# Forming layer 1's third adaLN group on VectorE behind the delta-rule stages instead of in layer 0's second feed-forward product

## The chip, the cores and the metric

The kernel is one program on one core of a Trainium2 chip. The metric is the device time of that core in microseconds, the median of three runs. Engines are called TensorE (PE in the rows, its weight loads PEld), VectorE (DVE), ScalarE (ACT), GpSimd (POOL) and SyncE (SP, which here only issues DMAs).

## The reference

One inference step through two trunk layers, on 128 context tokens and 512 latent tokens of width 1024, all in float32. Cut to what matters here:

```python
mod = (jax.nn.silu(cond) @ p['w_ada'] + p['b_ada'])[:, None, :]
sh1, sc1, gt1, sh2, sc2, gt2 = jnp.split(mod, 6, axis=-1)
h = rmsnorm(x, p['g_pre_mix']) * (1.0 + sc1) + sh1
...  # h @ w_in; gated delta rule, HGRN2 and latent attention side by side -> mix
x = x + gt1 * rmsnorm(mix @ p['w_out'], p['g_post_mix'])
h = rmsnorm(x, p['g_pre_ffn']) * (1.0 + sc2) + sh2
ff_a, ff_b = jnp.split(h @ p['w_ffn_in'], 2, axis=-1)
x = x + gt2 * rmsnorm((jax.nn.silu(ff_a) * ff_b) @ p['w_ffn_out'], p['g_post_ffn'])
```

`cond` is one vector for the latent tokens and one for the context. So `mod` is a product of two rows with a 1024 x 6144 matrix, 24 MB per layer. The kernel cuts it into three groups of 2048 columns: group 0 is sh1 and sc1, group 1 is gt1 and sh2, group 2 is sc2 and gt2.

## The kernel before

The residual stream is kept feature-major (128 partitions x 8 blocks x 640 tokens), and the tokens are worked in two halves of 320. Every large product is made of matmuls of 128 x 128 weights on 320 columns: a weight is split into a high and a low part in a reduced float32 format (ScalarE makes `wh`, VectorE `wl`, lines 632 and 633), and each 128 x 128 block costs three matmuls per half (line 656). Projections drain through two pairs of PSUM banks, tags g0 and g1.

The instructions are not ordered by hand. The code says what depends on what, and its order is a priority; a planner then simulates the engines, starts on each engine the ready instruction of the highest priority, and so fixes each engine's queue and the places of tiles in rings of buffers. `high_priority(offset=...)` lifts weights (WPRI) and some drains ahead of the code's order. On the chip each engine runs its queue strictly in order. A tile of tag "r" is a region of 128 x 2 x 640 float32; there are 12 of them (`BUFS`, line 39), and 8 of tag "h". A new tile waits until one of its tag is released.

A layer (`layer`, line 1371) runs its mixer first. `ORDER` (line 46) is `g0 g1 i0|2*e0 i1+L0|2*m0+e1 P0|f0 a0|m1+f1`: the two delta-rule halves (`gdn`, g0 and g1), the projections of the HGRN2 halves (i0, i1) and of the latent attention (L0), then the rest. In layer 1 the first HGRN half's tokens of half 0 are projected ahead of everything. A delta-rule half (`gdn_raw`, `gdn_main`) takes two region tiles (KQ and VT), forms its projections and convolutions (line 740), sends a triangular matrix through DRAM into another layout and back (lines 848 to 873), and then scans over chunks (lines 946 to 969), each step with small matmuls on TensorE and short operations on VectorE in turn. KQ lives until the scan's end, VT until the half's last step (`gdn_end`). `hgrn_in(1)` takes four region tiles (two for itself, two for the latent attention) if they haven't been taken. Then comes the output projection, the first feed-forward product (a seven-product scheme, line 563) and the second (w_ffo, pieces of both halves for the first four of eight output blocks, then half by half).

The adaLN groups are formed in two ways. `ada` uses TensorE, and `ada_vec` (line 269) uses VectorE: for each of four blocks j of 512 columns it loads eight weight tiles of 128 x 512, two to a DMA of 512 KB (four DMAs per block, line 293), into a ring of VRING = 2 tiles, and multiplies each by a per-partition scalar and adds it to an accumulator, for the two conditions in turn (line 297 the first, line 299 the other seven). Two accumulators of the same size alternate. `total` (line 279) then sums an accumulator over its 128 partitions with eight matmuls of one column, in two bursts; a float32 matmul makes two records. After the fourth block, `ada_end` makes the gains and gates. It is a generator that stops after each block; a block's `total` is written behind the next block's accumulation. Before the change, layer 0 forms its own groups 1 and 2 on TensorE (`GR`), and layer 1's group 0 too (`PE_NEXT`); layer 1's groups 1 and 2 (`VEC_NEXT`) go through `ada_vec` with "h" tiles, two blocks ahead of each of the first four output blocks of layer 0's second feed-forward product (line 1479).

Of the kernel before, what the change touches and what calls it, by code (L numbers as in the profile page):

```python
# [50 lines left out]
SPRI = 5000  # L51
NKEEP = 6
GR = ((1, 2), ())
PE_NEXT, VEC_NEXT = (0,), (1, 2)
VRING = 2
MPRI = 8000
HPRI = 0
# [109 lines left out]
class Builder:  # L167
# [1203 lines left out]
    def layer(self, l, h, pre):  # L1371
# [3 lines left out]
        inp = lambda n, halves=(0, 1): pre.pop(n) if n in pre else self.gemm(I["w_in"][l, n], hv, KD, halves)  # L1375
        filler = self.ada(l, GR[l], "c1", "w1", AD0) if GR[l] else iter(())
        fill = lambda n: [next(filler, None) for _ in range(n)]
        rb = lambda shape: self.blk(shape, tag="r")
        r2 = rb([128, 2, NT])
        self.mkab = r2[:, 1]  # L1380
# [10 lines left out]
        def gdn(pr):  # L1391
            self.use(f"c{pr}", f"w{pr}")
            gd[pr] = (rb([128, 2, NC, 64]), rb([128, 2, NT]))
            self.gdn_raw(l, pr, inp, *gd[pr])
            if pr == 0:
                fill(100)
            terms[pr] = self.gdn_main(l, pr, *gd[pr])

        def gdn_end(pr):
            self.use(f"c{pr}", f"w{pr}")  # L1400
            KQ, VT = gd[pr]
            yield from self.mix_out(VT[:, 0], terms[pr])
            mix[pr] = self.finish_mixer(VT[:, 0], VT[:, 1], self.vec[:, l, V_GNW:V_GNW + 1], f"w{pr}")
# [25 lines left out]
        def hgrn_end(pr):  # L1429
            self.use(f"c{pr}", f"w{pr}")  # L1430
            yield from self.mix_out(hs[pr][0][:, 0], terms[2 + pr])
            mix[2 + pr] = self.finish_mixer(hs[pr][0][:, 0], hs[pr][2], self.vec[:, l, V_HNW:V_HNW + 1], f"w{pr}")

        steps = {"g": gdn, "e": gdn_end, "i": hgrn_in, "m": hgrn, "f": hgrn_end, "L": lambda n: mla_in(), "P": lambda n: mla(),
                 "a": lambda n: self.attention(l, st[1], mix, range(4))}
        for group in ORDER.split():
# [187 lines left out]
```

## Time and profile before

| | |
|---|---|
| Median of 3 runs | 1977.1 us (1975.47 to 1982.02) |
| Profiled execution | 1979.4 us, span 1977.6 us, mean granted TensorE clock 0.99 |
| TensorE matmul, weight load | 97%, 88% of the span |
| VectorE, ScalarE, GpSimd | 69%, 50%, 1% |
| DMA | mean 115 GB/s; 32 loads of 512 KB for `ada_vec` |

Stages of the profiled execution: layer 0's mixer to about 500 us, its output projection and first feed-forward product to about 860, its second product to about 1062; layer 1's mixer to about 1458, its products to the end. Times in the rows are microseconds from the span's start, means of one instruction are nanoseconds. An engine that is busy need not be at its peak: matmuls are pipelined and their ends are modelled, so that a matmul which waits inside the array looks longer. The granted clock is a share of TensorE's full 2.4 GHz.

### The profile page before, as it was taken

What the parts mean: (1) busy time and instruction counts of PE and PEld (TensorE: products, weight loads), DVE (VectorE), ACT (ScalarE), POOL (GpSimd) and SP (SyncE); (2) the same over time, 40 slices, a digit from 0 to 9 for tenths busy, and PEclk for the clock granted to TensorE, in tenths of its full rate; (3) what the DMA queues carried; (4) which work ended last, traced back from release to release, by engine and by line L of the source; (5) the groups of instructions that cost most, each with busy time, mean ns of one, the idle gap of its engine ahead of it and who ended that gap; (6) DMA issues with size and microseconds to landing.
All of it is one profiled execution on the core that took longest, in us unless ns stands there. A gap on an engine that the chain in (4) does not pass through costs nothing. (4 is left out here: it accounts for less than half of the span.)

```text
span 1977.6 us, 40034 instructions
## 1 busy us (share of the span) xinstructions
PE 1910.7 (97%) x15688; PEld 1739.2 (88%) x15688; DVE 1370.9 (69%) x2962; ACT 997.1 (50%) x2086; POOL 16.2 (1%) x64
## 2 busy tenths in 40 slices
PE   6999999999999999999999999999999999999996
PEld 3748888888999979999998987888899999999996
DVE  5537567696677757788887786678756977776245
ACT  4515253754676435551355551648457755555243
POOL 0000000000000000000000000000000000000000
PEclk9999999999999999999999999999999999999998
DMA  9652211210554452256764232112036532223344
GB/s 320 207 183 64 59 42 28 58 37 18 187 176 150 139 166 85 86 167 202 235 192 133 62 100 52 29 42 58 5 100 187 167 117 86 86 86 103 87 139 141
DMA packets 157486, 226.56 MB, mean 115 GB/s; under 512 B 38769, under 2 KB 65521, under 8 KB 157297
## 3 DMA queue, kind: packets, MB, share of 16 engines
q1 hardware_dynamic: 156656, 222.70, 36.8%
q8 instruction: 123, 2.02, 0.4%
q0 software_dynamic: 640, 1.31, 0.3%
q14 instruction: 67, 0.54, 0.1%
HBM read 209.99 MB, written 12.65 MB: 113 GB/s over the span
## 5 line engine op out<-in xcount | busy, mean ns | idle before, releaser
L632 ACT ACTIVATE wh<-raw 128x512 fp32r<-128x512 f32 (+2 forms) x634 | 391.0, 617 | 603.8 <-PE g L656 413.5
L633 DVE TENSOR_TENSOR wl<-raw,wh 128x512 fp32r<-128x512 f32 (+1 forms) x610 | 408.2, 671 | 303.4 <-ACT wh L632 265.9
L656 PE MATMUL g<-h,wh 128*128 128x320 f32 x2448 | 541.4, 319 | 8.6 <-ACT h L481 3.3
L656 PEld LDWEIGHTS g<-h,wh 128*128 128x128 f32 x2448 | 401.3, 189 | 41.0 <-issue 16.2
L656 PE MATMUL g<-h,wl 128*128 128x320 f32 x1224 | 338.3, 316 | 0.5 <-DVE wl L633 0.5
L656 PE MATMUL g<-w,wh 128*128 128x320 f32 x1152 | 246.1, 314 | 5.5 <-ACT r L1448 5.5
L656 PEld LDWEIGHTS g<-h,wl 128*128 128x128 f32 x1224 | 218.4, 189 | 12.0 <-issue 6.4
L656 PEld LDWEIGHTS g<-w,wh 128*128 128x128 f32 x1152 | 191.0, 191 | 6.2 <-ACT r L1448 6.0
L656 PE MATMUL g<-r,wh 128*128 128x320 f32 x768 | 165.5, 313 | 0.0
L656 PE MATMUL g<-w,wl 128*128 128x320 f32 x480 | 132.7, 314 | 0.0
L563 PE MATMUL g<-h,wh 128*128 128x320 f32 x768 | 129.0, 310 | 0.0
L656 PEld LDWEIGHTS g<-r,wh 128*128 128x128 f32 x768 | 127.5, 190 | 0.6
L563 PEld LDWEIGHTS g<-h,wh 128*128 128x128 f32 x768 | 116.3, 188 | 3.6 <-issue 3.4
L557 DVE TENSOR_TENSOR raw<-raw,raw 128x512 f32<-128x512 f32 x128 | 88.0, 687 | 2.2
L656 PEld LDWEIGHTS g<-w,wl 128*128 128x128 f32 x480 | 87.4, 192 | 0.2
L563 PE MATMUL g<-w,wh 128*128 128x320 f32 x512 | 85.9, 310 | 0.0
L563 PE MATMUL g<-r,wh 128*128 128x320 f32 x512 | 85.5, 309 | 0.0
L299 DVE SCALAR_TENSOR_TENSOR h<-h,silu_c,h 128x512 f32<-128x512 f32 x112 | 78.5, 745 | 4.6 <-DMA h<-in_w_ada_dram 4.5
L563 PEld LDWEIGHTS g<-w,wh 128*128 128x128 f32 x512 | 77.6, 188 | 3.4 <-ACT r L575 3.4
L656 PE MATMUL g<-r,wl 128*128 128x320 f32 x288 | 79.3, 312 | 0.0
L563 PEld LDWEIGHTS g<-r,wh 128*128 128x128 f32 x512 | 77.7, 188 | 0.0
L563 PE MATMUL g<-h,wl 128*128 128x320 f32 x384 | 71.9, 309 | 0.0
(378 smaller groups left out, 3094.8 us busy)
## 6 DMA issues: line engine op xcount, KB each, us to landing
raw<-in_w_ffi_dram SPq DMA_DIRECT2D x224, 256.0 KB
raw<-in_w_ffo_dram SPq DMA_DIRECT2D x120, 256.0 KB
raw<-in_w_in_dram SPq DMA_DIRECT2D x106, 256.0 KB
w<-in_w_ada_dram SPq DMA_DIRECT2D x96, 256.0 KB
raw<-in_w_out_dram SPq DMA_DIRECT2D x64, 256.0 KB
h<-in_w_ada_dram SPq DMA_DIRECT2D x32, 512.0 KB
r<-in_w_ada_dram SPq DMA_DIRECT2D x32, 256.0 KB
r<-in_xT_dram SPq DMA_DIRECT2D x6, 640.0 KB
```

What stands on the lines that cost most here:

```text
L299: nc.vector.scalar_tensor_tensor(out=acc[:, s], in0=raw[:, k % 2], scalar=c, in1=acc[:, s], op0=ALU.mult, op1=ALU.add)
L557: nc.vector.tensor_tensor(out=o, in0=a, in1=b, op=ALU.add)
L563: nc.tensor.matmul(ps, lhsT=w[e][:, k], rhs=a[f][:, k], start=first and i == 0, stop=i == 11, skip_group_check=not first)
L632: self.nc.scalar.activation(hi, src, AF.Copy)
L633: self.nc.vector.tensor_tensor(out=lo, in0=src, in1=hi.bitcast(F32), op=ALU.subtract)
L656: self.nc.tensor.matmul(ps[h], lhsT=w[:, k], rhs=rhs(e, kk, h), start=(kk == 0 and i == 0), stop=(kk == nk - 1 and i == 2))
```

## The change

Layer 1's group 2 leaves `VEC_NEXT` and is formed inside layer 1's own mixer, by the same `ada_vec`, with tiles of tag "r" in place of "h" and PSUM of tag c1 in place of c0. The generator is advanced by two blocks behind the first delta-rule half's `gdn_main`, and to its end behind the second's. As the generator makes its tiles at its first step, they come behind the tiles of the first half and before those of the second in the code's order. No arithmetic changes.

```diff
 GR = ((1, 2), ())
-PE_NEXT, VEC_NEXT = (0,), (1, 2)
+GV = ((), (2,))
+PE_NEXT, VEC_NEXT = (0,), (1,)
 VRING = 2
@@
         fill = lambda n: [next(filler, None) for _ in range(n)]
+        slow = self.ada_vec(l, GV[l], "c1", "r") if GV[l] else iter(())
         rb = lambda shape: self.blk(shape, tag="r")
@@
             terms[pr] = self.gdn_main(l, pr, *gd[pr])
+            for _ in range((2, 100)[pr]):
+                next(slow, None)
```

## Rows read from the trace of the kernel before

**Rows 1.** The page: engines' busy us, and the chain that ended last

```profile
PE 1910.7 (97%) x15688; PEld 1739.2 (88%) x15688; DVE 1370.9 (69%) x2962; ACT 997.1 (50%) x2086; POOL 16.2 (1%) x64
...
PE 27%; DVE 2%; ACT 1%; issue 1%; DVEq 0%; ACTq 0%
```

**Rows 2.** PE, PEld, DVE, ACT, POOL busy us (instructions), clock, DMA, GB/s

```profile
870.00:1005.00 135.00, 131.94 (x907) 130.13 (x906) 113.69 (x196) 35.74 (x68) 0.00 (x0) 0.98 0.70 218
1100.00:1300.00 200.00, 194.54 (x2185) 167.71 (x2185) 143.68 (x359) 94.10 (x200) 3.59 (x9) 1.00 0.22 56
1195.00:1237.00 42.00, 42.00 (x426) 32.99 (x428) 26.24 (x99) 6.82 (x14) 0.00 (x0) 1.00 0.20 50
...
1808.50:1943.50 135.00, 134.98 (x919) 134.56 (x918) 53.71 (x91) 46.90 (x88) 0.00 (x0) 1.00 0.43 125
```

**Rows 3.** The same view for the matmuls of line 656 alone

```profile
870.00:1005.00 135.00, 119.74 (x779) 0.98 0.70 218
...
1808.50:1943.50 135.00, 134.58 (x917) 1.00 0.43 125
...
1195.00:1237.00 42.00, 30.63 (x145) 1.00 0.20 50
```

**Rows 4.** Lines that form groups; timeline rows: start, us, operation, count

```profile
L299 DVE SCALAR_TENSOR_TENSOR h<-h,silu_c,h x112: 739/744/754, 871.1 to 1001.3; 128x512 f32<-128x512 f32 x112
...
L282 DVE TENSOR_TENSOR mods<-m,vec x8: 155/157/167, 888.5 to 1004.1; 128x8 f32<-128x8 f32 x8
...
L293 SPq DMA_DIRECT2D h<-in_w_ada_dram x32: 367/368/427, 848.5 to 993.5; - x32
...
891.44 3.39 DVE L299 SCALAR_TENSOR_TENSOR h<-h,silu_c,h 128x512 f32<-128x512 f32 x5
...
935.75 0.88 DVE L297 TENSOR_SCALAR h<-h,silu_c 128x512 f32<-128x512 f32 x2
```

**Rows 5.** TensorE's timeline around one burst, and its waits from 945 to 1010

```profile
983.08 1.02 PE L279 MATMUL m<-onet,h 128*128 128x1 f32 x8 [0.42 <-DVE h L299]
983.96 0.54 PE L656 MATMUL g<-r,wh 128*128 128x320 f32 x2
...
PE m L279 <- DVE h L299: 1.3, 3, 0.7
```

**Rows 6.** TensorE alone behind two bursts: busy us (matmuls), granted clock

```profile
919.00:923.00 4.00, 4.00 (x19) 0.59 0.72 236
...
1003.50:1008.00 4.50, 4.50 (x23) 0.62 0.21 58
```

**Rows 7.** ScalarE's timeline, first drains of the second HGRN half

```profile
1183.05 0.77 ACT L671 ACTIVATE r<-g 128x320 f32<-128x320 f32 x2
...
1198.01 0.77 ACT L671 ACTIVATE r<-g 128x320 f32<-128x320 f32 x2
```

**Rows 8.** Timelines: last statistic, a convolution; line 949 of the first scan

```profile
1062.64 0.81 PE L445 MATMUL m<-w,onesD 128*128 128x320 f32 x2 [0.47 <-DVE w L441]
...
1130.92 0.88 DVE L740 SCALAR_TENSOR_TENSOR w<-w,vec,w 128x642 f32<-128x642 f32 x1
...
L949 DVE SCALAR_TENSOR_TENSOR st_r<-m,eg,r x20: 272/276/284, 1196.0 to 1233.9; 128x64 f32<-128x64 f32 x20
```

**Rows 9.** Stretches as in rows 2; gap: length less DVE

```profile
1065.00:1120.00 55.00, 52.77 (x347) 48.93 (x347) 35.19 (x73) 31.59 (x74) 2.16 (x12) 0.94 0.19 55
1120.00:1190.00 70.00, 67.46 (x541) 61.58 (x541) 58.68 (x122) 38.08 (x88) 1.74 (x3) 1.00 0.33 84
1190.00:1212.00 22.00, 21.21 (x338) 16.68 (x335) 14.09 (x48) 4.70 (x10) 0.00 (x0) 1.00 0.17 49
1212.00:1237.00 25.00, 25.00 (x262) 19.77 (x264) 14.41 (x59) 2.56 (x5) 0.00 (x0) 1.00 0.25 59
```

**Rows 10.** The chain of waits, a run of small matmuls

```profile
1378.21 1.47 PE m L1040 x32
```

**Rows 11.** VectorE's timeline, layer 1, the first use of G2

```profile
1502.45 2.87 DVE L514 SCALAR_TENSOR_TENSOR w<-w,G,w 128x320 f32<-128x320 f32 x6 [1.56 <-ACT w L407]
```

## The prediction

> **What bounds the kernel now.** I read the engine totals first: TensorE is busy for 97% of the span, VectorE for 69%, and the chain of work that ended last is almost all matmul [rows 1]. Whatever moves VectorE work can therefore pay only where TensorE waits for VectorE, and can cost where it makes TensorE wait. Next come the stretches of the table by stage [rows 2]: 870 to 1005 us is the part of layer 0's second feed-forward product beside which groups 1 and 2 of layer 1 are formed; 1808.5 to 1943.5 is the same product in layer 1 with no such work beside it; 1100 to 1300 holds layer 1's two delta-rule stages and 1195 to 1237 the state scan of the first. Matmuls of the product alone in the first two, of equal length, are 779 and 917 [rows 3]. At 135 us / 917 = 0.147 us each, the forming of two groups takes 138 x 0.147 = 20.3 us of TensorE's time. Half of that is what the change touches. The delta-rule stretch has TensorE busy for 194.5 of 200 us, but it is looser than that: the scan's 145 projection matmuls fill 30.6 us [rows 3] where 145 x 0.147 = 21.3 would do. VectorE is busy for 113.7 of 135 us in the first stretch and 143.7 of 200 in the stages that shall take the work [rows 2].
>
> **Part 1, what leaves the feed-forward product.** Group 2 is half of the 112 + 16 VectorE operations [rows 4]. Five of the long ones in a row take 3.39 us, so each follows the last by (3.39 - 0.745)/4 = 0.66 us; two of the short ones take 0.88, 0.44 each. With seven small ones of 0.16 (line 282 four times and three gains and gates) that is 56 x 0.66 + 8 x 0.44 + 1.1 = 41.6 us of VectorE. With it go half of the 32 loads of 512 KB, and the small sums over partitions of line 279. VectorE is not the engine that ends this stretch, so its 41.6 us alone give nothing. What lies on TensorE is this. Each of a group's four blocks has two bursts of eight records; a burst begins at 983.08 and the next matmul at 983.96 [rows 5], 0.88 us. 8 x 0.88 = **7.0 us** go. TensorE waits for VectorE ahead of these bursts, **1.3 us** from 945 us on [rows 5]. And behind the last burst the granted clock is 0.62 from 1003.5 to 1008 (the level of 1.2 GHz for most of it): 23 matmuls where 4.5/0.147 = 30.6 fit, so 7.6 x 0.147 = **1.1 us**; the same followed group 1's third block at 919 [rows 6], and that one stays. Sum: -9.4 us.
>
> **Part 2, what the delta-rule stages get.** The same 7.0 us of bursts arrive there. TensorE's queue is in order and 97% busy, so I take the whole: **+7.0**, with bounds 0 (all of it in the scan's looseness above) and 7.0. The waits ahead of the bursts come along: **+1.3**, bounds 0 and twice that, 2.6, since here the scan's own VectorE operations stand in the queue too. For a half-clock stretch I take 0 (the clock is 1.00 from 1100 to 1300 [rows 2]), at most 1.1.
>
> The loads: 16 issues of 0.37 us on SP's queue [rows 4], among the projection weights and the delta rule's round trip through DRAM (lines 848 to 873). The stretch moves 56 GB/s and 8.4 MB over 200 us add 42, against 218 in the stretch that they leave [rows 2], so the transfers cost nothing. A load that waits for its ring tile holds everything behind it on SP for at most one tile's four operations, 2.7 us; the weights have seven buffers of lead, the round trip has none. I take 0, upper bound 2.7 for each of two round trips that run while the sums are formed.
>
> The VectorE operations between the scan's steps: the planner lets a ready operation start in any gap. An operation of 0.66 us holds a scan step back by 0.33 on average. Ten steps with three hand-overs each are 30 places, so 10 us at most if every place is hit, and nothing as long as TensorE has projection matmuls to run meanwhile. I take **+1**, bounds 0 and 10.
>
> **The region buffers.** The tag "r" has 12 buffers. At the first projection of the second HGRN half (i1) they hold r2, hg, hs0 (2), the delta rule's KQ and VT of both halves (4): 8, and i1 takes the last four. After the change the slow sums hold four from before the second half's KQ and VT are made until they end, so all 12 are taken and i1's first two tiles must wait for a release. It wants them at 1183.1 and at 1198.0 us [rows 7]. When do they come free? Nothing but tiles and loads holds the sums back, so I let them start when the product has given up its tiles, some us behind its last statistic at 1062.6, and fill VectorE's gaps. That the planner fills gaps ahead of program order, the rows show: a convolution of the second half (line 740) runs at 1130.9, and the first half's scan, which the code writes earlier (line 949), from 1196.0 [rows 8]. The gaps are 19.8 us from 1065 to 1120, 11.3 to 1190, 7.9 to 1212, 10.6 to 1237 [rows 9]. Three blocks (31 us) fit by about 1190, when the first accumulator comes free, and all four (41.6) by about 1218. i1's first tile is thus late by 7 us and the second, when a ring tile is done with, by about 15. TensorE feels this only when both pairs of PSUM banks (tags g0, g1) are full: with the first projection drained at about 1190 the third can run, and the fourth waits some us for the second to drain. I take **+2**. Lower bound 0, for a later tile gives nothing back. Upper bound: the scan runs with no projection beside it. Then the 21.3 us of projection wait, the scan shrinks to 42 - 21.3 = 20.7 us, of which its own 426 - 145 = 281 small records [rows 2, 3], at 1.47/32 = 0.046 us each [rows 10], fill 12.9; 7.8 us of TensorE are lost.
>
> The group's results are first used in layer 1 at line 514, at 1502 us [rows 11], 280 us after they would be done: nothing.
>
> **Sum.** -9.4 + 7.0 + 1.3 + 1 + 2 = +1.9 us. The profiled execution took 1979.4 us (span 1977.6), 2.3 above the median of 1977.1; so 1981.3 for a run like it, and 1979.0 as a median.
>
> **Rivals.** A measurement of this kernel can tell about 0.3%, 5.9 us, from no change.
>
> A, slower: the buffers decide. If the third block isn't done by about 1205, no tile comes free, both bank pairs are full from 1197 and TensorE has only the scan. That happens if VectorE's gaps are fewer than I count, as blocks 3 and 4 stand behind the second delta-rule half, beside which VectorE is busy for 58.7 of 70 us from 1120 to 1190 [rows 9]. Price: 7.8 us (above) and up to 8 more, as the scan then has no cover for the operations between its steps (24 of 0.33). -9.4 + 8.3 + 7.8 to 15.8 = +6.7 to +14.7, **about 1988**. For it: 16 tiles want 12 places. Against: the first release suffices, and KQ goes when the scan ends in any case. The Trainium skill's Perfetto Trace Analysis, section Optimization Strategy, says that a gap that keeps returning on the engine that should be saturated can mean that there isn't room for the next tile. No such gap is in the trace before the change; by that rule the change would make one. Chance 0.30.
>
> B, faster: the bursts and their waits fall into the looseness of the scans (30.6 us of matmul time for 21.3 of work). Then -9.4 stays nearly whole, **about 1969**. For it: the weight loads fill 167.7 of 200 us in the delta-rule stretch and 130.1 of 135 in the product [rows 2]. Against: TensorE can't jump over an instruction that waits. The Trainium skill's Perfetto Trace Analysis, section Identifying the Most-Contended Engine, says to judge TensorE's room by the busy share of its weight loads and not by that of its matmuls; by that rule 16% of this stretch would be free and the 8.3 us would vanish. The trace agrees that the matmul share hides some slack, as the counts show, but not that a burst can use it. Chance 0.20.
>
> C, the change doesn't do what it says: the sums wait for nothing but tiles, so the planner draws them ahead of the delta-rule stages, to 1065 to 1120, where VectorE has 19.8 us of gaps beside norm and gates, and the rest is done before i1 asks at 1183. No hold, no scan disturbed: -9.4 + 8.3 = -1.1, **1976**. Against: 41.6 us don't fit into 31.1. Chance 0.10.
>
> **How the numbers follow.** Forecast 0.40, A 0.30, B 0.20, C 0.10. The range of 80% reaches from 1968 (B with a little less than all hidden) to 1990 (A without its last third); it leaves out some 0.08 on either side. Faster by over 0.3% (below 1971.2): most of B and a tail of the forecast, 0.20. Slower (above 1983.0): A and a tail of the forecast from its open bounds, 0.34. Within: 0.46.
>
> **What would show it.** In the product from 945 to 1005: no line 299 or 279, about 69 matmuls in 10 us, no stretch at the lower clock at 1004. Layer 1's first projection about 9 us earlier. Line 299 with "r" tiles in layer 1: if its third block ends by 1205 (on the old clock) the forecast holds, if all end before 1183 it is C; if the third block runs on into the end of the first scan and TensorE's projection matmuls in that scan are far fewer than 145, it is A. If the bursts appear in the scans and the stretch from the first projection to the attention doesn't grow by 7 us, it is B. I am wrong altogether if the planner reorders something else, such as the conversion of weights, by more than these few us.

## The result and the profile after

| | before | after |
|---|---|---|
| time, median (lowest to highest), us | 1979.6 (1975.5 to 1984.3) | 2011.3 (2007.8 to 2011.7) |
| ratio, 95% interval | 1 | 1.0149 (1.0133 to 1.0165) |
| profiled span, us | 1977.6 | 2006.0 |

The change makes the kernel slower by 1.5%. The prediction said 1979.0, with 1990 as its upper end, so both the time and the range were wrong. Differences in us below are (ratio - 1) x 1979, with the interval worked out likewise, so the change is +29.5 (26.3 to 32.7). One profiled execution can stand several us from the next: the last statistic of layer 0's product, up to which e7 and e13 (below) run the same code, ends at 1048.1 us in the one and at 1057.2 in the other.

After the change TensorE has as many matmuls as in [rows 1] and is busy longer, at a smaller share. Line numbers of after are one higher up to line 1378. From the page of the changed kernel:

```profile
PE 1918.9 (96%) x15688; PEld 1749.0 (87%) x15688; DVE 1373.9 (68%) x2962; ACT 999.3 (50%) x2086; POOL 16.3 (1%) x64
```

To see where the time is, cut layer 1's mixer at its events. In the changed kernel these are the switch of ScalarE's table at the end of the gates (1095.6), the first scan (1196.1 to 1228.0), the second scan (1266.1 to 1301.8) and the last projection drained (1391.2). Columns as in [rows 2]:

```profile
1095.60:1196.10 100.50, 86.00 (x777) 78.26 (x777) 85.91 (x163) 44.78 (x94) 3.68 (x12) 0.92 0.44 128
1196.10:1228.00 31.90, 20.83 (x234) 15.34 (x231) 26.60 (x96) 4.12 (x14) 0.00 (x0) 0.55 0.18 47
1228.00:1266.10 38.10, 37.34 (x569) 33.34 (x571) 23.39 (x49) 22.35 (x41) 0.00 (x0) 0.91 0.17 40
1266.10:1301.80 35.70, 35.70 (x532) 29.38 (x528) 27.07 (x91) 10.85 (x24) 0.00 (x0) 1.00 0.08 26
1301.80:1391.20 89.40, 85.13 (x791) 74.99 (x791) 62.10 (x135) 51.27 (x116) 1.47 (x2) 0.94 0.21 61
```

The same five stretches in the kernel that leaves the group out (e5 below), which has the change's gain and none of its work in the mixer:

```profile
1096.00:1180.00 84.00, 80.96 (x770) 72.60 (x768) 64.52 (x134) 47.65 (x106) 3.59 (x9) 1.00 0.31 79
1180.00:1218.20 38.20, 38.20 (x357) 29.88 (x357) 25.49 (x97) 6.40 (x13) 0.00 (x0) 1.00 0.18 52
1218.20:1241.10 22.90, 22.65 (x481) 20.22 (x480) 12.58 (x24) 14.76 (x28) 0.00 (x0) 1.00 0.13 27
1241.10:1284.90 43.80, 42.52 (x518) 35.24 (x519) 33.00 (x99) 20.48 (x43) 0.00 (x0) 1.00 0.11 31
1284.90:1346.80 61.90, 59.68 (x708) 50.61 (x707) 47.93 (x108) 43.36 (x96) 1.47 (x2) 1.00 0.18 53
```

Both start within half a microsecond of each other. From there the changed kernel needs 295.6 us, the other 250.8. Of the 44.8 us between them, TensorE's idle time (length less PE busy) is 30.6 - 6.8 = 23.8, and 21.0 is TensorE being busy longer. The totals' own time is 7.0 of that; for the rest there is the granted clock. A mean between 0.5 and 1 mixes the two levels, so a stretch of length T at mean c spends 2(1 - c)T at 1.2 GHz: 16.1 + 28.7 + 6.9 + 0 + 10.7 = 62 us in the changed kernel, none in the other.

Three things are seen in the trace of after. **The first scan has no projections beside it**: line 657's matmuls, 145 in [rows 3], are none from 1190 to 1220, and i1's drains, at 1183 and 1198 in [rows 7], begin at 1227.57, as that scan ends and its KQ comes free.

```profile
1190.00:1220.00 30.00, 0.00 (x0) 0.00 (x0) 0.62 0.18 44
1220.00:1240.00 20.00, 3.34 (x11) 2.04 (x11) 0.64 0.14 38
```
```profile
1227.57 0.77 ACT L672 ACTIVATE r<-g 128x320 f32<-128x320 f32 x2 [16.07 <-PE m L947]
```

**The totals run behind the second scan.** From TensorE's timeline: the second and third follow the second scan's last product (line 955), though the third block's sums end at 1220. The accumulators are held until these totals have run, and the fourth block's sums come only behind them (to 1325).

```profile
1302.02 0.45 PE L955 MATMUL m<-st_r,w 64*64 64x64 f32 x8
1302.39 1.95 PE L280 MATMUL m<-onet,r 128*128 128x1 f32 x16
...
1305.01 2.29 PE L280 MATMUL m<-onet,r 128*128 128x1 f32 x16
```

**VectorE's sums stand between the links of a chain.** From VectorE's timeline: lines 867 and 869 are the elimination that inverts the delta rule's triangular matrix, 30 short operations each of which needs the one before. The planner put a sum of 0.74 us (or one of the short ones) between every two of the first 24.

```profile
1145.79 0.27 DVE L869 TENSOR_TENSOR w<-w,w 80x120 f32<-80x120 f32 x1
1145.98 0.74 DVE L300 SCALAR_TENSOR_TENSOR r<-r,silu_c,r 128x512 f32<-128x512 f32 x1
...
1147.54 0.28 DVE L867 TENSOR_TENSOR w<-w,w 80x126 f32<-80x126 f32 x1
1147.74 0.74 DVE L300 SCALAR_TENSOR_TENSOR r<-r,silu_c,r 128x512 f32<-128x512 f32 x1
1148.40 0.28 DVE L869 TENSOR_TENSOR w<-w,w 80x126 f32<-80x126 f32 x1
1148.60 0.74 DVE L300 SCALAR_TENSOR_TENSOR r<-r,silu_c,r 128x512 f32<-128x512 f32 x1
```

In e5, where nothing stands between two links, they start 0.3 us apart:

```profile
1143.77 0.28 DVE L870 TENSOR_TENSOR w<-w,w 80x120 f32<-80x120 f32 x1
1144.09 0.28 DVE L872 TENSOR_TENSOR w<-w,w 80x120 f32<-80x120 f32 x1
1144.40 0.27 DVE L870 TENSOR_TENSOR w<-w,w 80x110 f32<-80x110 f32 x1
```

The first half's chain starts within 2 us of e5's and ends 15 us later; the two rows, of after and of e5, carry the first and last start. That is as much as the earlier start had given.

```profile
L869 DVE TENSOR_TENSOR w<-w,w x15: 178/246/281, 1133.5 to 1166.7; 80x30 f32<-80x30 f32 x2, 80x56 f32<-80x56 f32 x2, 80x78 f32<-80x78 f32 x2, 80x96 f32<-80x96 f32 x2
```
```profile
L872 DVE TENSOR_TENSOR w<-w,w x15: 179/253/282, 1132.2 to 1151.2; 80x30 f32<-80x30 f32 x2, 80x56 f32<-80x56 f32 x2, 80x78 f32<-80x78 f32 x2, 80x96 f32<-80x96 f32 x2
```

### The profile page after: what moved, and what is told of

The parts are those of the page before. It is cut to its first block, busy times and chain, and to the rows that moved or that the text cites. A ratio compares the mean times of both kernels' runs of the same rounds, so it can differ in the third digit from the quotient of the medians.

```text
span 2006.0 us, 40042 instructions
## 1 busy us (share of the span) xinstructions
PE 1918.9 (96%) x15688; PEld 1749.0 (87%) x15688; DVE 1373.9 (68%) x2962; ACT 999.3 (50%) x2086; POOL 16.3 (1%) x64
## 5 line engine op out<-in xcount | busy, mean ns | idle before, releaser
L657 PE MATMUL g<-h,wl 128*128 128x320 f32 x1224 | 342.6, 317 | 0.5 <-DVE wl L634 0.5
L657 PEld LDWEIGHTS g<-h,wl 128*128 128x128 f32 x1224 | 220.4, 190 | 12.2 <-issue 6.6
L564 PE MATMUL g<-h,wl 128*128 128x320 f32 x384 | 71.9, 309 | 0.0
L564 PEld LDWEIGHTS g<-h,wl 128*128 128x128 f32 x384 | 60.3, 188 | 0.0
```

Of the source, the lines that this page charges most:

```text
L564: nc.tensor.matmul(ps, lhsT=w[e][:, k], rhs=a[f][:, k], start=first and i == 0, stop=i == 11, skip_group_check=not first)
L657: self.nc.tensor.matmul(ps[h], lhsT=w[:, k], rhs=rhs(e, kk, h), start=(kk == 0 and i == 0), stop=(kk == nk - 1 and i == 2))
```

## The experiments

The first theory was that the hold is the whole loss: the totals wait for their PSUM tile of tag c1, which the second half cycles until its scan ends, so i1 has no tiles. The rivals were VectorE's time, and the loads. (The expectations speak of 128 additions; 128 is both groups. The change, and each experiment with the sums, has 64: 56 long and 8 short, or 64 long.)

### Taking the hold away: e1, e2, e3

```
e1   for _ in range((100, 0)[pr]):                    # was (2, 100): all blocks behind the first half
e2   slow = self.ada_vec(l, GV[l], "g", "r")          # was "c1": the totals' PSUM tag
e3   slow = self.ada_vec(l, GV[l], "c1", "r", 1, 1)   # one accumulator, one load tile, total at once
```

> The only edit: all four blocks of the slow sums are written behind the first half's delta-rule stage and none behind the second's, so that all four bursts of totals stand in TensorE's order ahead of the second half's use of the PSUM tag c1. VectorE has the same 128 additions to do as in the changed kernel. Theory 1 (the accumulators and loads keep four region tiles until the totals get a PSUM tile, which in the changed kernel is behind the second scan, at 1302 us, and TensorE has no projection work meanwhile): the bursts run when the sums are ready, the tiles come free at about 1180 to 1230 us, most of the 44 us lost in the mixer comes back, and the time is 1965 to 1985. Rival 2 (VectorE's 128 additions of 0.66 us, which stand ahead of the convolutions and between the steps of the scan, are what costs): the additions are as many and stand even earlier, so the time stays at 2000 or above.

Measured: 2008.7 us, +26.9 (20.6 to 33.2).

> The only edit: the totals of the slow sums take their PSUM tile from tag g instead of c1. The pace (two blocks behind the first half, the rest behind the second) and everything else stays as in the changed kernel. Theory 1 in its narrow form (it is the PSUM tag c1 that the second half's delta-rule stages cycle which keeps the totals back): totals 1 to 3 run when their block is summed, before 1240 us instead of at 1302 to 1325, and the time falls to 1970 to 1990. If the place in TensorE's order is what keeps them back, not the PSUM tile, totals 1 to 3 stay behind the second scan and the time stays at 2005 to 2015. Rival 2 (VectorE's additions): 2000 or above, with the totals early all the same.

Measured: 2019.2 us, +36.8 (31.1 to 42.5).

> The only edit: the slow sums keep two region tiles instead of four (one accumulator, one tile for the loads), and each block's total stands directly behind its own sums. The pace is that of the changed kernel, VectorE's work is the same, and totals 2 and 3 still stand behind the second half. Theory 1: two tiles stay free for the projections of the second recurrence, TensorE has work in the first scan again, and 15 to 40 of the 44 us lost in the mixer come back: 1970 to 1996. Rival 2 (VectorE's additions): 2000 or above. Rival 3 (one load tile makes VectorE wait for each load, and the sums run longer): above the changed kernel's 2011.

Measured: 2013.9 us, +33.6 (26.7 to 40.8).

The totals did come early in e1 and e2 (their last matmul starts at 1214 in e1, at 1228 in e2, not at 1327), and in e2 the PSUM tag is all that differs, so c1 was what kept them back. But the tiles did not come free in time for the first scan: line 657 has 36 matmuls in it in e1 and none in e2, where [rows 3] has 145. So these two runs don't show what the hold is worth. Only in e3 did the first scan have its projections again (132 matmuls of line 661, TensorE busy throughout it, clock 1.00). Line 657 in the first scan of e1, then of e2, then all of TensorE's work in that of e3:

```profile
1201.80:1243.40 41.60, 7.53 (x36) 5.46 (x36) 0.68 0.05 16
```
```profile
1184.10:1215.10 31.00, 0.00 (x0) 0.00 (x0) 0.68 0.15 33
```
```profile
1196.40:1238.10 41.70, 41.70 (x409) 33.43 (x410) 31.23 (x94) 10.98 (x27) 1.41 (x3) 1.00 0.24 64
```

Not one of the three gave the time back, and by e3 the first theory falls as the whole account. What these runs have besides is a wait of TensorE, whose queue is in order, for VectorE: in e1 and e2 for the sums, and in e1 and e3, 7.3 and 8.7 us at a time, for the copies that follow the first half's elimination (line 890 of e1, 894 of e3). TensorE's waits for the sums up to the first scan, in e1 and then in e2:

```profile
PE m L280 <- DVE r L300: 8.0, 2, 6.9
```
```profile
PE m L280 <- DVE r L300: 6.9, 1, 6.9
```

### Each part alone: e4, e5, e6, e12, e13

e4 and e6 are built on the kernel before, e12 and e13 on e5, which leaves group 2 of layer 1 out. All use the change's places (two steps behind the first half, the rest behind the second).

```
e4   held = [self.blk([128, 2, 512], tag="r") for _ in range(4)]   # behind gdn(0); read behind gdn(1)'s scan
e5   VEC_NEXT = (1,)                                               # mods of group 2 = bias
e6   for each of 4 blocks, 16 times: scalar_tensor_tensor(out=t[:, 0], in0=t[:, 1], scalar=c, in1=t[:, 0], ...)
e12  e5 + 16 loads into two "r" tiles, a 4-column addition each
e13  e5 + 4 totals (8 matmuls, 16 records each, over a tile of zeros, tag c1)
```

> Built on the kernel before: the third group stays in the feed-forward product, and nothing is summed in the mixer. Four region tiles are taken behind the first half's delta-rule stage, touched by a four-column write, and given back only behind the second half's last scan step (four small additions read them together with its result). Their only effect is that the four tiles are not to be had meanwhile. Theory 1 (the hold alone makes the loss): 20 to 44 us above the kernel before, 1999 to 2022, with the projections of the second recurrence late and a granted clock below 0.9 in 1150 to 1250 us. Rivals 2 and 3 (VectorE's additions, or the loads and bursts in the mixer, make it): 1977 to 1985.

Measured: 1991.1 us, +11.3 (8.1 to 14.4). That lies between the two expectations: the hold costs something, and not the whole.

> Built on the kernel before, with the third group of layer 1 left out altogether: the product sums one group instead of two, the mixer sums nothing, and layer 1's third-group gains come from the bias alone. What it leaves out is that group's 1024-term sums, so its time is that of the change's gain without its cost. The prediction's term for the product was -9.4 (1968 to 1971 here); the changed kernel's trace has layer 1 start 13.5 to 15.4 us earlier, which gives 1962 to 1966.

Measured: 1963.1 us, -15.0 (-17.8 to -12.1).

> Built on the kernel before: the group stays in the product. VectorE gets 128 additions of the same shape as the change's at the same two places (64 behind the first half's delta-rule stages, 64 behind the second's), on one region tile that is written once and used by nothing else: no loads, no totals, one tile held instead of four. Theory 2, as it stands now that the hold alone was worth 12 us (VectorE's additions ahead of the second half's convolutions and scan steps make the larger part): 15 to 30 us above the kernel before, 1994 to 2009, with TensorE idle and its granted clock below 1 ahead of the first scan. If instead the totals that TensorE waits for, or the loads, make it: 1978 to 1986.

Measured: 1995.7 us, +17.4 (13.9 to 21.0).

> Built on the kernel with the group left out (1963): only the 16 loads of 512 KB come back in the mixer, into two region tiles, at the change's places (half behind the first half's delta-rule stages, half behind the second's); a four-column addition per load frees the tile. No sums, no totals. The third group's gains still come from the bias alone. If the loads (SP's queue, two tiles held, shared bandwidth) are a term of the 31 us that the narrowed kernels cost: 1970 to 1990. If they cost nothing, as the prediction put it: 1961 to 1966.

Measured: 1968.9 us, a ratio of 0.9955 (0.9940 to 0.9971) to before, +6.1 over e5, with 4.1 either way. It misses both expectations, between them. In the profiles 2.8 us of the difference between e12 and e5 stand ahead of 866 us (a switch of ScalarE's table at 865.8 and at 863.0), before anything that the edit touches, so the loads themselves may cost less.

> Built on the kernel with the group left out (1963): only the four totals come back in the mixer, 64 matmuls over one region tile that is written once with zeros, with their four small additions of the bias, one of them behind the first half's delta-rule stages and three behind the second's. No loads and no sums (the group's sums are left out). The prediction's term is +7: 1968 to 1972. If the bursts fall into TensorE's looseness: 1961 to 1966. If their place in TensorE's queue costs more than their own time: above 1975.

Measured: 1978.5 us, a ratio of 0.9994 (0.9982 to 1.0005), +13.9 over e5, with 3.7 either way.

The parts add up: -15.0 + 17.4 (sums) + 13.9 (totals) + 11.3 (hold) + 6.1 (loads) = +33.7, with about 8 either way, against +29.5 measured. So the loss is four costs of 6 to 17 us each, as each is alone, against one gain of 15. The other way round it doesn't hold for the hold: e3, and e9 below, ease it in the changed kernel and don't get its price back.

**The hold**, in e4: the first scan with four tiles taken and nothing else changed. All of TensorE's work, and then line 656's matmuls alone (7 of them, where [rows 3] has 145 in a stretch of this kind):

```profile
1193.80:1222.60 28.80, 18.74 (x227) 13.98 (x227) 22.07 (x92) 1.58 (x4) 0.00 (x0) 0.60 0.06 18
```
```profile
1193.80:1222.60 28.80, 1.41 (x7) 0.88 (x7) 0.60 0.06 18
```

The scan is 9.4 us shorter than its 38.2 us with projections, and the projections come behind it.

**The totals**, in e13: three of four stand together behind the second scan. TensorE's timeline there, and its granted clock (in the last but two columns):

```profile
1295.28 1.95 PE L1389 MATMUL m<-onet,r 128*128 128x1 f32 x16
1297.08 0.39 PE L656 MATMUL g<-h,wh 128*128 128x320 f32 x1
1297.41 0.54 PE L1040 MATMUL m<-w,w 64*64 64x64 f32 x6
1297.87 3.57 PE L1389 MATMUL m<-onet,r 128*128 128x1 f32 x16
1301.37 0.47 PE L1040 MATMUL m<-w,w 64*64 64x64 f32 x2
1301.77 3.57 PE L1389 MATMUL m<-onet,r 128*128 128x1 f32 x16
```
```profile
1294.00:1296.00 2.00, 2.00 (x21) 1.74 (x21) 1.11 (x4) 0.00 (x0) 0.00 (x0) 1.00 0.20 72
1296.00:1298.00 2.00, 2.00 (x19) 1.72 (x19) 0.40 (x3) 0.00 (x0) 0.00 (x0) 0.91 0.00 0
1298.00:1300.00 2.00, 2.00 (x10) 2.00 (x11) 0.00 (x0) 0.00 (x0) 0.00 (x0) 0.50 0.00 0
...
1308.00:1310.00 2.00, 2.00 (x38) 2.00 (x36) 1.90 (x7) 0.83 (x2) 0.00 (x0) 0.50 0.00 0
1310.00:1312.00 2.00, 2.00 (x52) 2.00 (x51) 0.22 (x2) 0.00 (x0) 0.00 (x0) 0.68 0.00 0
```

A burst of 16 records takes 1.95 us at the full clock. Behind the first the clock falls to 0.50 and stays there for some 13 us, although TensorE is busy all the time: each later burst takes 3.57, and the delta rule's products between and behind them run at the lower level too, until it comes back at 1311 in a run of such products. The other total, alone at 1109 between projections, took 1.84 us, and the clock stayed at 1.00.

**The sums**, in e6: the elimination chain of the first half. Its 15 starts of line 868 reach over 27.4 us, against 19.0 in e5 (above).

```profile
L868 DVE TENSOR_TENSOR w<-w,w x15: 183/254/281, 1144.5 to 1171.9; 80x30 f32<-80x30 f32 x2, 80x56 f32<-80x56 f32 x2, 80x78 f32<-80x78 f32 x2, 80x96 f32<-80x96 f32 x2
```

There is more behind it than those 8.4 us. VectorE has hardly any idle time in that stretch before the change, as the first row shows (19.98 of 20.70 us busy, in the kernel before), so whatever is added there pushes the rest back. The second half's convolutions, last begun at 1149.1 us before, are last begun at 1180.7 in e6; TensorE waits 5.2 us for what follows them, the longest of its waits ahead of the first scan. And between the two scans, the second and third row (before and e6), the second half's stages take 49.2 us instead of 22.8.

```profile
1145.60:1166.30 20.70, 18.43 (x127) 15.23 (x126) 19.98 (x52) 12.97 (x27) 1.74 (x3) 1.00 0.25 75
1234.20:1257.00 22.80, 22.43 (x481) 20.12 (x479) 12.69 (x23) 14.70 (x28) 0.00 (x0) 1.00 0.14 28
```
```profile
1244.50:1293.70 49.20, 43.62 (x677) 40.29 (x676) 41.95 (x93) 31.05 (x62) 0.00 (x0) 1.00 0.16 39
```

No run separates the two, the links of a chain drawn apart and a VectorE that is simply full, so how the 17.4 divide between them stays open.

### Without VectorE's time: e7, e9

```
e7   nc.vector.scalar_tensor_tensor(out=acc[:, s, :16], in0=raw[:, k % 2, :16], scalar=c, in1=acc[:, s, :16], ...)
e9   e7 with range((100, 0)[pr])
```

> The changed kernel with every addition cut from 512 columns to 16: it leaves out the sums of the other columns. Loads, the four region tiles, their hold until behind the second scan, the totals, the bursts and the number of VectorE instructions stay. What goes is nearly all of VectorE's time in them. Theory 2: the convolutions are on time again, and only the gain in the product and the price of the hold are left: 1979 - 14 + 12, so 1970 to 1985. If the instructions' places and waits rather than VectorE's time are what costs: 1995 to 2010.

Measured: 1994.8 us, +16.6 (11.9 to 21.6).

> The narrowed kernel (additions over 16 of 512 columns, the sums of the others left out) with all four blocks behind the first half instead of two: loads, 16-matmul totals and their bursts stay, VectorE's time is gone, and the four region tiles come free as soon as the loads are through, before the second half's stages. What should be left of the price is the bursts. Theory (hold and VectorE's time are the two large terms, bursts the third): 1963 + 7, so 1967 to 1975. If the narrowed kernel's 31 us over the kernel with the group left out are not from the hold to behind the second scan but from loads, totals and their places in the queues: 1985 to 1998.

Measured: 1994.0 us, +15.0 (9.9 to 20.4).

e7 is 31.7 over e5, which is what loads, totals and hold cost alone (6.1 + 13.9 + 11.3 = 31.3). Its expectation of 1970 to 1985 missed because it knew only the hold's price. e9 misses too. Its totals have run by 1206 and line 660 has 69 matmuls in its first scan, half of what [rows 3] has, but TensorE now waits for the totals, and the narrow sums in turn for the loads, of which the last is issued at 1193. TensorE's first wait before the scan:

```profile
PE m L283 <- DVE r L303: 5.5, 3, 3.5
```

### Other places, other engines: e8, e11, e14, e15

```
e8   nc.gpsimd.tensor_scalar_mul(tmp[:, s], raw[:, k % 2], c); nc.gpsimd.tensor_tensor(out=acc[:, s], ...)
e11  e6 with range((0, 100)[pr])
e14  in the output projection: if s == 0 and n in (0, 2, 4, 6, 7): next(slow, None)
e15  e14, one block ahead of the attention, the rest at n in (0, 2, 4, 6)
```

> The kernel with the additions alone (128 additions beside an unchanged product, one region tile, +17 us), with all 128 written behind the second half's delta-rule stages and none behind the first's. If it is the place ahead of the second half's convolutions that costs, the convolutions are on time and the rest is hidden beside scans and projections: 1978 to 1986. If VectorE's 85 us cost wherever they stand in the mixer: 1990 to 2002.

Measured: 1994.3 us, +15.4 (11.5 to 19.4). The sums cost as much behind the second half, where the convolutions are on time (last begun at 1146.2), so late convolutions are not needed for the price. Beside the scans TensorE now waits for VectorE's steps in them (3.5 us at line 964, 2.1 at 954); that these are chains as well fits, and doesn't prove that the chain is what makes the price.

> The same group, formed in the mixer by GpSimd instead of VectorE (a multiplication and an addition for each of VectorE's operations), with three region tiles, one block behind each step of the mixer and each block's total behind the next step. VectorE does only the four small additions of the bias. Theory 2 (VectorE's time is the larger part of the price): 1966 to 1982, a version that could beat both. If three tiles held through the mixer cost as much as four held to behind the second scan, 1978 to 1985; if TensorE waits at the totals because GpSimd's blocks are long, above 1990. How long GpSimd takes for one such operation no row so far shows.

Measured: 2081.3 us, +103.1 (100.1 to 106.3). GpSimd's operations take 1.90 and 1.48 us (this engine's spans are rough in the profile), and TensorE waits for them at the totals, 35.1 us in two waits:

```profile
L321 POOL TENSOR_SCALAR r<-r,silu_c 128x512 f32<-128x512 f32 x56 | 106.0, 1903 | 11.8 <-DMA r<-in_w_ada_dram 11.8
L322 POOL TENSOR_TENSOR r<-r,r 128x512 f32<-128x512 f32 x56 | 81.7, 1479 | 0.0
```

The Trainium skill's GPSIMD Engine Reference, section Engine selection, puts GpSimd at about half VectorE's speed for operations with two inputs and calls one input “roughly line-rate”. The first agrees (1.48 against VectorE's 0.74 us, in a form that multiplies as well, in [rows 4]). The second isn't borne out here: 1.90 us against the 0.44 of VectorE's one-input form in [rows 4].

> The same group, formed by VectorE later still: beside the first half of layer 1's output projection, one block behind every second of its eight columns, with the accumulators and load tiles in the same region buffers. The mixer is as with the group left out. VectorE is idle 37 of 100 us there and the sums take 41.6, and the group is first used at the end of that stretch. With the gain of 15 in the product, 7 for the bursts and up to 10 for a later first use: 1965 to 1985, and it may beat both kernels; if weights' conversion on VectorE comes late for the projection, above 1985.

Measured: 1996.3 us, +19.0 (16.0 to 22.0). In the trace the sums run on to 1526 us, so the group's first use is late; from 1500 to 1540 TensorE is busy for 21.0 of 40 us, at 0.62 of the clock, and 11.8 of the idle time are one wait for the sums at a total. No delta-rule chain stands beside the sums here, and forming the group costs 34.0 us over e5 all the same.

> As the kernel with the sums beside the output projection, with the first block one step earlier, ahead of the attention, and the others one column pair earlier, so that the last total is not behind the end of the first half. If the late first use was what cost there, this is faster than it by up to 10 us; if VectorE's time beside attention is as dear as in the delta-rule stages, slower.

Measured: 1995.1 us, +17.4 (14.1 to 20.6). One block earlier changes nothing that can be told, though TensorE now waits only 1.9 us at the totals, so the late first use was not shown to be what cost in e14.

### The clock by itself, and the bursts apart: e10, e16

```
e10  for _ in range(2): nc.tensor.matmul(p[:, 128:256], lhsT=self.onesD, rhs=self.ident, ...)   # first scan
e16  kernel before; two matmul pairs of a total behind every WK row blocks, one output column later
```

> The changed kernel with work added for TensorE alone: two matmuls of 128x128 whose result nobody reads, behind each of the scan's steps' first and second products, in layer 1's first scan (38 places at most, 76 matmuls). They keep TensorE busy while the scan waits for VectorE and no projection can run. If the lower clock is a cost of its own, the granted clock in that scan rises from its 0.55, the scan and the projections behind it get shorter, and the time falls by 4 to 15 us, to 1996 to 2007. If the clock only follows the starvation and costs nothing that the scan would not wait for anyway, the time stays at 2008 to 2016, or rises by up to 15 us for the added work.

Measured: 2029.1 us, +49.5 (43.5 to 55.4). That is above both expectations. The clock didn't rise: it was 0.50 for the whole first scan, with TensorE busy for 44.2 of 50.6 us, and with 76 added records of 0.42 us the scan takes 50.6 us where it took 31.9.

```profile
1196.30:1246.90 50.60, 44.15 (x306) 32.88 (x302) 29.51 (x106) 4.11 (x14) 0.00 (x0) 0.50 0.11 30
```

So how much of the loss in the scan the lower clock makes by itself stays open.

> Built on the kernel before: both groups stay in layer 0's second feed-forward product, and nothing is summed in the mixer. The one edit: a block's total is no longer 16 matmuls in one burst right behind the next block's sums, but pairs of two, set between the product's groups of four row blocks one output column later (four accumulators instead of two). The bursts' own 14 us stay. If a burst costs more than its own time through the lower clock behind it and the wait ahead of it, as the runs of the mixer say, the time is 1970 to 1976, faster than both kernels; if the clock falls behind single pairs as well, or the weight loads of the pairs break the product's rhythm, 1978 to 1986.

Measured: 1981.8 us, a ratio of 1.0009 (0.9996 to 1.0022). The time is in the second range, but the planner put the pairs together again, mostly eight records at a time, and the waits ahead of them stayed (2.9 us, before 3.0). The edit didn't do what it was to do, and whether spread totals would be cheaper is open. No version was found that beats the kernel before.

## Why the prediction was wrong

**Part 1, the product: -9.4 predicted, -15.0 (12.1 to 17.8) measured.** The direction and the bursts were right. The waits were right too: 3.0 us before and 1.3 in e5, so 1.7 went where 1.3 were forecast. The term that is missing is the norm between the product and the mixer, which the sum left out. Before the change, the first row, TensorE is idle for 3.8 us from 1061.5 to 1111, at a mean clock of 0.93; in e5, the second, the like stretch has 1.7 us, at 1.00. That is 2.1 us less idle time and, by 2(1 - c)T, some 7 us less at 1.2 GHz, of which about half is lost: an estimate of 5 to 6 us, about what is missing. Why the norm goes better without the group stays open.

```profile
1061.50:1111.00 49.50, 45.73 (x308) 42.65 (x307) 33.37 (x70) 24.41 (x60) 0.31 (x6) 0.93 0.24 73
```
```profile
1046.00:1096.00 50.00, 48.35 (x338) 44.29 (x337) 35.96 (x76) 25.94 (x63) 0.32 (x6) 1.00 0.26 84
```

**Part 2, the bursts: +7.0 with 7.0 as the bound, +13.9 measured.** 64 records at 0.88 us for eight were right. What failed is the term beside it, "For a half-clock stretch I take 0 ..., at most 1.1": e13 shows some 13 us at 1.2 GHz behind three bursts that stand close together, which costs about half of that. [rows 6] had shown the fall behind bursts in the product. The bound came from one of those, and a clock of 1.00 in a stretch that had no bursts said nothing on what they would do there. The waits ahead of the bursts, +1.3, came out: 1.0 us in the changed kernel.

**VectorE between the steps: +1, bounds 0 and 10; +17.4 measured.** This is the step that failed most. The gaps of [rows 9] were treated as free time and only the scan as a chain. The 11.3 us of gaps from 1120 to 1190 are not where the sums went: in the 20.7 us of the first half's elimination (lines 866 and 868) VectorE was idle for 0.7. The elimination is a chain too, and a planner that puts 0.66 us where two links would follow each other after 0.3 draws it apart. What VectorE has to do behind it, the second half's convolutions, comes later (the last by 31.6 us in e6). "Nothing as long as TensorE has projection matmuls" failed with it: in e6 TensorE is idle for 11.9 us from 1096 to 1196, against 3.8 before, though projections were still to come.

**The buffers: +2, upper bound 7.8; +11.3 measured.** "When the first accumulator comes free" was taken for the end of the sums. It is the end of the totals, whose PSUM tile the second half's stages keep until 1302. I had followed the region tag and not the PSUM tag of the same generator.

**The loads: 0, upper bound two times 2.7 = 5.4; +6.1 (2.0 to 10.2) measured**, near the bound. Its mechanism was not looked into further.

**The rivals.** Rival A named the right sign and one right mechanism, and its sign was borne out: the third block runs on until 1220 and the scan has no projections. By the Trainium skill's Perfetto Trace Analysis, section Optimization Strategy, which that rival cited, such gaps can mean that there is no room for the next tile; e4 agrees, with 10.1 us of idle in its first scan. A's price of +6.7 to +14.7 lacked VectorE's term and the clock. B fell: by e13, the bursts don't vanish in the looseness, whatever the share of the weight loads. C fell: the first sum is at 1103, not at 1065.

**The shape of the error.** Three of four costs (VectorE's operations, the buffers, the loads) were taken near their lower bounds because a piece of slack seemed to cover each: VectorE's gaps, projections beside the scan, free tiles. In the changed kernel the hold took the projections from beside the scan. The fourth, the totals, stood at its upper bound, and the bound lacked the clock. So the forecast of near no change failed in several terms at once, and not in one.

## What to carry to other kernels

An engine's idle time summed over a stretch is not room: ask where in the stretch it lies, and look for chains of short operations that need each other before filling it. When work moves, follow every ring that it holds, PSUM tags as well as SBUF tags, up to the instruction that releases it, and ask where that stands in its engine's queue. And price each part alone by a kernel that has only that part: here four such runs added up to the whole within their intervals.

## What the runs showed of the hardware

In e13 TensorE's granted clock fell from full to 1.2 GHz (1.00 to 0.50 from one stretch of 2 us to the next but one) with the engine busy for all of the time; what it did just before was a burst of 16 matmul records with one column each, and two more such bursts followed in the 13 us or so at the lower level. Behind the lone burst at 1109 it stayed at 1.00. In e10 it stayed at 1.2 GHz through a scan in which TensorE was busy for 87% of the time. In these runs a busy share near 1 was therefore no sign of the full clock; the clock has to be read beside it.
